# A layer norm's scale and bias on the vector engine instead of GpSimd, and an expert's selection ahead of two subtractions

## The chip, the cores and the metric

The kernel runs on one core of a Trainium2 chip. The metric is the device time of one execution in microseconds (us); the time of a kernel is the median of its runs. The engines are TensorE (PE; PEld is its weight load), VectorE (DVE, here the vector engine), ScalarE (ACT), GpSimd (POOL) and SyncE (SP, which issues most loads).

## The reference, cut to what matters

Two transformer blocks with two layers each are computed one after the other in float32, on 256 tokens of 1024 features. The change touches the second block. Its layer norms, after the residual has been added, and its expert layer are:

```python
for layer in range(DEPTH):
    y = mixer_block(x, ...)
    x = layer_norm(DN_ALPHA * x + y, ln_g[layer, 0], ln_b[layer, 0])
    y = swiglu_2(x, ...) if layer % 2 == 0 else moe_ffn(x, ...)
    x = layer_norm(DN_ALPHA * x + y, ln_g[layer, 1], ln_b[layer, 1])
```

Ahead of the second block the first one ends with an RMS norm with the scale `final_g`. The expert layer routes each token to the best two of 8 experts (hidden width 1408).

## The kernel before, in words

**Split products.** Each float32 product is made of three: every operand is split into a high part, rounded by a cast, and a low part, the difference. For a weight piece, loaded by SyncE into one of the `raw` buffers, the scalar engine makes the high part `whi` (line 233) and the vector engine the low part `wlo` (line 236); in the expert layer each sixth low part is made by GpSimd (`lo_pool = 6`). TensorE then issues the products of lines 342 (high with high), 343 (low weight) and 344 (low state).

**The x state** is a tile `xstate` of 128 x 2 x 1024, two "tokens" t of 128 tokens each. `close` (lines 1624 to 1629) adds the residual, takes the statistics and normalises x in place. What follows reads x in two ways. First, `pre(t)` makes the operand of the next product: `to_feat` turns x by TensorE (line 395), applies the norm's scale and bias by column to the turned tile (line 416 on the vector engine for features 0 to 511, line 412 on the scalar engine for the rest), casts the high parts `xh` (line 388 on the vector engine, line 386 on the scalar engine) and subtracts for the low parts `xl` (line 389). Second, `tok(t)` multiplies x itself by the scale (line 1645) and adds the bias (line 1646), both on GpSimd with rows broadcast to all partitions, for the residual at the end of the layer. The final norm of block 1 has only a scale (line 1696).

**When tok runs.** In `moe` the flag `now` is set and `tok(t)` is issued in `pre(t)`. Otherwise it is put off: `put_off` is a generator in a list of background work, of which the long products (`gemm_tok`) take a step from time to time. The order within each engine's queue is written by a scheduler that goes by priority and by when it thinks inputs are ready; `high_priority` raises what is issued in it, and `issue_after(i)` makes the instructions of a block follow i in the queue of i's engine. `pieces` uses it with `self.made`, the last instruction of the latest `pre`, to keep the weights' splits behind the state's.

There are four places: the mixer of layer 0 (line 1696, put off), the feed-forward of layer 0, the mixer of layer 1 (both lines 1645 and 1646, put off) and the expert layer of layer 1 (the same lines, `now`).

**The expert layer** (`moe`) takes the state's operands, computes the router's logits (line 1757, line 1761), picks the best two (lines 1763 to 1767), ranks the chosen tokens per expert (lines 1770 to 1773, result `rk`), and then stores the split of x as `xth` and `xtl` (lines 386 and 389) for the gather. For an expert e, `gather(e)` compares the ranks with the numbers 1 to 128 (line 1817, the selection `G`) and multiplies `xth` and `xtl` by `G` on TensorE (line 1824). Expert 0 is gathered at once, the others as background work. The list `last` says behind which vector instruction the low part of each stored token is queued; `self.behind` does the same for the first expert's weight splits:

```python
last[0] = last[1]
last[1] = ranked
for t in range(2):
    with tc.issue_after(last[t].ins), tc.issue_after(evac[t].ins):
        self.split(xth[:, t], xtl[:, t], self.x[:, t].rearrange("p (q k) -> p k q", k=KD))
self.behind = last[1]
```

Of the kernel before, what the change touches and what calls it, by code (L numbers as in the profile page):

```python
# [11 lines left out]
F32R = mybir.dt.float32r  # L12
# [3 lines left out]
OP = mybir.AluOpType  # L16
# [3 lines left out]
P = 128  # L20
D = 1024
KD = 8
# [62 lines left out]
class Net:  # L85
# [1547 lines left out]
    def gain(self, L, which, pool, xp, tag="lnb", bufs=2, now=False):  # L1633


        nc, a = self.nc, self.a
        g, b = a["ln_g_2"][L, which], a["ln_b_2"][L, which]
        gb, bb = (self.bcast(v, pool, f"lnb{L}{which}{i}", D, tag=tag, bufs=bufs) for i, v in enumerate((g, b)))
        gf, bf = (self.sp.tile([P, KD], F32, name="lnf", tag="lnf", bufs=4) for _ in range(2))
        nc.gpsimd.dma_start(gf, g.rearrange("(p k) -> p k", k=KD))  # L1640
        nc.gpsimd.dma_start(bf, b.rearrange("(p k) -> p k", k=KD))

        def tok(t):
            z = self.x[:, t]
            nc.gpsimd.tensor_tensor(out=z, in0=z, in1=gb, op=OP.mult)
            nc.gpsimd.tensor_tensor(out=z, in0=z, in1=bb, op=OP.add)

        def pre(t):
            z = self.x[:, t]
            last = self.to_feat(z, KD, xp[t][0], xp[t][1], lambda k: (gf[:, k:k + 1], bf[:, k:k + 1]))  # L1650
            if now:
                tok(t)
            return last
        if not now:
            self.rest = self.put_off(tok)
        return pre

    @staticmethod
    def put_off(tok):
        for t in range(2):  # L1660
            tok(t)
            yield

    def mix_consts(self):
# [20 lines left out]
    def block2_layer0(self):  # L1685
        nc, a, tc = self.nc, self.a, self.tc
        xp = self.xparts()
        fg = self.feat(a["final_g"], self.cp, "final_g")

        def final(pool, xp, tag, bufs):  # L1690
            gb = self.bcast(a["final_g"], pool, "fgb", D, tag=tag, bufs=bufs)

            def pre(t):
                z = self.x[:, t]
                return self.to_feat(z, KD, xp[t][0], xp[t][1], lambda k: (fg[:, k:k + 1], None))
            self.rest = self.put_off(lambda t: nc.gpsimd.tensor_tensor(out=self.x[:, t], in0=self.x[:, t], in1=gb, op=OP.mult))
            return pre
        with ExitStack() as es:
            self.block2_mixer(0, xp, final, es)
            pool = es.enter_context(tc.tile_pool(name="f2", reuse_waits="tile", bufs=1))  # L1700
            xp = self.xparts()
            pre = self.gain(0, 0, pool, xp)
            self.later(iter(range(6)), self.rest)
            lhs = lambda k, t: (xp[t][0][:, k], xp[t][1][:, k])
            w1, w3 = (a[n][0].rearrange("(p k) n -> p k n", k=KD) for n in ("ffn_w1_2", "ffn_w3_2"))
            self.swiglu_tok(lhs, lambda c0, cw: w1[:, :, c0:c0 + cw], lambda c0, cw: w3[:, :, c0:c0 + cw],
                            lambda c0, cw: a["ffn_w2_2"][0][c0:c0 + cw, :].rearrange("(p k) n -> p k n", p=P), 2816, pool,
                            self.close(), pre=pre, nxt=(self.w_in(1), 768, 1024))
            self.extend()
        self.x2parts = self.xparts()  # L1710
        self.load_vec(1)
# [19 lines left out]
    def moe(self, xp, pre, loads, pool):  # L1731

        nc, a, tc = self.nc, self.a, self.tc
        alpha = (2 * 2) ** 0.25
        out = self.dump["x2_1"] if self.out is None else self.out.rearrange("o s d -> (o s) d")
# [3 lines left out]
        tri, iota, rhl, rb = loads  # L1739
        one = self.ones5[:, 0:1]  # L1740
        nc.vector.memset(one, 1.0)
        top2, top, sel, rk, cmb, rkb_ = self.by_expert
# [7 lines left out]
        last, evac = [], []  # L1750
# [14 lines left out]
        for t in range(2):  # L1765
# [6 lines left out]
        nc.tensor.matmul(prk[:, E:2 * E], tri, sel[:, 1], start=False, stop=True)  # L1772
        ranked = nc.vector.scalar_tensor_tensor(out=rk, in0=prk[:, :2 * E].rearrange("p (t e) -> p t e", t=2), scalar=1.0, in1=sel,
                                       op0=OP.add, op1=OP.mult)
        last[0] = last[1]
        last[1] = ranked

        xth, xtl = (pool.tile([P, 2, KD, P], F32R, name=n) for n in ("xth", "xtl"))
        for t in range(2):
# [24 lines left out]
        def experts(base):  # L1804
            rkb = rk
            if base:
                rkb = rkb_
                nc.vector.tensor_scalar(out=rkb, in0=rk, scalar1=-float(base), scalar2=None, op0=OP.add)
            w1, w3 = ([[a[n][0, e].rearrange("(p k) n -> p k n", k=KD)] for e in range(E)] for n in ("exp_w1_2", "exp_w3_2"))
            w2 = [[a["exp_w2_2"][0, e].rearrange("(p k) n -> p k n", p=P)] for e in range(E)]  # L1810
            G, gx, st = {}, {}, {}

            def gather(e):

                G[e] = self.xp.tile([P, 2, P], F32R, name="G", tag="xp", bufs=4)
                for t in range(2):
                    nc.vector.tensor_scalar(out=G[e][:, t], in0=iota, scalar1=rkb[:, t, e:e + 1], scalar2=None, op0=OP.is_equal)
                gh, gl = gx[e] = [pool.tile([P, KD, P], F32R, name=n, tag=n, bufs=2) for n in ("gh", "gl")]
                for k in range(0, KD, 4):
                    for i, (x, d) in enumerate(((xth, gh), (xtl, gl))):  # L1820
                        pg = self.mi().rearrange("p (k n) -> p k n", k=4)
                        for j in range(4):
                            for t in range(2):
                                nc.tensor.matmul(pg[:, j], x[:, t, k + j], G[e][:, t], start=t == 0, stop=t == 1)  # L1824
                        if i:
                            nc.vector.tensor_copy(d[:, k:k + 4], pg)
                        else:
                            nc.scalar.copy(d[:, k:k + 4], pg)
                    yield
# [96 lines left out]
            for e in range(E + 1):  # L1926
                if e < E:
                    if e == 0:
                        for _ in gather(0):
                            pass  # L1930
                        if not base:
                            weights()
                    if e + 1 < E:
                        self.later(gather(e + 1))
                    gs = st["g", e] = pool.tile([P, H], F32, name="gs", tag="gs", bufs=2)
                    up(e, w1, lambda t, b, bw, ps: nc.scalar.activation(gs[:, b:b + bw], ps, AF.Silu),
                       (w2[e - 1], 0, D) if e else (w3[e], 0, H))
                    self.behind = None
                self.finish()
                if e:  # L1940
                    down(e - 1, (w3[e], 0, H) if e < E else None)
                    if e < E:
                        self.later(scatter(e - 1))
                if e < E:
                    self.later(weigh(e))
                    up(e, w3, lambda t, b, bw, ps: nc.vector.tensor_tensor(out=gs[:, b:b + bw], in0=ps, in1=gs[:, b:b + bw],
                                                                           op=OP.mult),
                       (w1[e + 1], 0, H) if e + 1 < E else (w2[e], 0, D))
                    self.finish()
                    self.later(turn(e))  # L1950
            finish()

        stats = [self.sp.tile([P, 2, 6], F32, name="bnst", tag="bnst") for _ in range(2)]
        experts(0)
        _, (most,) = nc.values_load_multi_w_load_instructions(ci[0:1, 0:1], min_val=0, max_val=256)
        with tc.If(most > P):
            experts(P)
# [69 lines left out]
```

## Time and profile before

| | us |
|---|---|
| median of 3 runs | 2438.66 |
| lowest, highest run | 2431.98, 2439.13 |
| profiled execution, its own time | 2432.68 |
| its span | 2430.9 |

In the profiled execution TensorE's granted clock is 0.964 of full speed on average. The profile's page gives for each engine its busy time; its chain of waits goes back from the last instruction to what released it. A timeline row is: start in us, duration in us, engine, line, operation, output<-inputs, shape, count, and in brackets the idle time before it with the instruction that ended it. A row with a count over 1 merges neighbours, and its duration runs from the first one's start to the last one's end.

### The profile page before, as it was taken

The numbers are of one execution on the slowest core, as the hardware profiler recorded it, in microseconds if no ns is written. First come the engines' busy times: TensorE is split into PE (matmuls) and PEld (weight loads), VectorE is DVE, ScalarE is ACT, GpSimd is POOL, SyncE is SP. The second block draws the span as 40 slices with busy tenths as digits, with TensorE's granted clock in tenths as the row PEclk, the third lists the DMA queues.
The fourth block names the chain that finished last, engine by engine and source line by source line (L and its number), as shares of the span: only waits on it lengthen the run. The fifth ranks groups of instructions, "written<-read, shape, count | busy, mean of one in ns | idle before, by whom it ended". The sixth has DMA issues, their size and how long they took to land.

```text
span 2430.9 us, 32300 instructions
## 1 busy us (share of the span) xinstructions
PE 2324.5 (96%) x12726; PEld 1875.9 (77%) x12726; DVE 1483.8 (61%) x2473; ACT 1069.6 (44%) x1700; POOL 309.4 (13%) x245
## 2 busy tenths in 40 slices
PE   8999999999998999999999989989999979999996
PEld 4667887777886778978787768968887768888885
DVE  4248742332357565567465775567566778898787
ACT  3127432222234544434353344423353347777774
POOL 1100000000002010003100210022101222232222
PEclk8989999999999999999998999999999979999998
DMA  8561244454423055644243454634243539889893
GB/s 300 182 191 36 87 156 146 146 183 143 132 83 108 26 180 178 201 138 162 97 139 141 132 185 161 210 112 169 86 155 132 180 127 340 324 317 327 313 343 135
DMA packets 121504, 419.40 MB, mean 173 GB/s; under 512 B 10992, under 2 KB 16112, under 8 KB 110592
## 3 DMA queue, kind: packets, MB, share of 16 engines
q1 hardware_dynamic: 114128, 401.32, 47.0%
q0 software_dynamic: 4832, 15.34, 2.3%
q8 instruction: 102, 1.67, 0.3%
q10 hardware_dynamic: 2384, 0.59, 0.1%
q14 instruction: 58, 0.48, 0.1%
HBM read 416.15 MB, written 1.07 MB: 172 GB/s over the span
## 4 chain that ended last, share of the span: by engine, by line
PE 83%; DVE 9%; issue 3%; POOL 2%; ACT 1%; DMA 1%; SPq 0%; POOLq 0%; ACTq 0%; DVEq 0%
PE acc L342 18%; PE acc L343 18%; PE acc L344 18%; PE acc L375 4%; PE acc L376 3%; PE acc L377 3%; DVE wlo L236 2%; PE mi L1055 2%; PE mi L528 2%; PE mi L540 2%; PE mi L1373 2%; PE mi L395 1%; PE mi L1824 1%; PE mi L1011 1%; PE mi L1039 1%
## 5 line engine op out<-in xcount | busy, mean ns | idle before, releaser
L236 DVE TENSOR_TENSOR wlo<-raw,whi 128x1024 fp32r<-128x1024 f32 (+3 forms) x661 | 797.8, 1234 | 508.0 <-ACT whi L233 502.6
L233 ACT CAST whi<-raw 128x1024 fp32r<-128x1024 f32 (+5 forms) x708 | 675.9, 994 | 710.1 <-PE acc L344 512.4
L342 PE MATMUL acc<-whi,xh 128*128 128x512 f32 (+3 forms) x1184 | 465.4, 396 | 11.6 <-ACT whi L233 4.8
L343 PE MATMUL acc<-wlo,xh 128*128 128x512 f32 (+3 forms) x1184 | 456.8, 386 | 13.1 <-DVE wlo L236 12.8
L344 PE MATMUL acc<-whi,xl 128*128 128x512 f32 (+3 forms) x1184 | 454.0, 384 | 2.2 <-DVE xl L389 2.2
L342 PEld LDWEIGHTS acc<-whi,xh 128*128 128x128 f32 x1184 | 228.4, 193 | 62.5 <-issue 12.0
L343 PEld LDWEIGHTS acc<-wlo,xh 128*128 128x128 f32 x1184 | 227.7, 192 | 55.5 <-DVE wlo L236 21.7
L344 PEld LDWEIGHTS acc<-whi,xl 128*128 128x128 f32 x1184 | 227.4, 192 | 38.3 <-DVE xl L389 3.7
L344 PE MATMUL acc<-whi,hl 128*128 128x512 f32 x528 | 207.6, 393 | 2.2 <-DVE hl L389 2.2
L342 PE MATMUL acc<-whi,hh 128*128 128x512 f32 x528 | 208.1, 394 | 0.0
L343 PE MATMUL acc<-wlo,hh 128*128 128x512 f32 x528 | 207.9, 394 | 0.0
L236 POOL TENSOR_TENSOR wlo<-raw,whi 128x1024 fp32r<-128x1024 f32 (+1 forms) x47 | 119.1, 2534 | 322.2 <-ACT whi L233 322.2
L342 PE MATMUL acc<-whi,gh 128*128 128x512 f32 (+1 forms) x384 | 148.3, 386 | 1.5 <-DVE yl L1886 1.4
L375 PE MATMUL acc<-xh,whi 128*128 128x512 f32 (+1 forms) x384 | 147.0, 384 | 0.0
L376 PE MATMUL acc<-xl,whi 128*128 128x512 f32 (+1 forms) x384 | 145.6, 380 | 0.0
L377 PE MATMUL acc<-xh,wlo 128*128 128x512 f32 (+1 forms) x384 | 145.3, 380 | 0.0
L344 PE MATMUL acc<-whi,gl 128*128 128x512 f32 (+1 forms) x384 | 144.9, 377 | 0.0
L343 PE MATMUL acc<-wlo,gh 128*128 128x512 f32 (+1 forms) x384 | 144.4, 376 | 0.0
L342 PEld LDWEIGHTS acc<-whi,hh 128*128 128x128 f32 x528 | 100.2, 190 | 25.6 <-issue 3.4
L344 PEld LDWEIGHTS acc<-whi,hl 128*128 128x128 f32 x528 | 100.3, 190 | 23.5 <-DVE hl L389 2.6
L343 PEld LDWEIGHTS acc<-wlo,hh 128*128 128x128 f32 x528 | 100.1, 190 | 20.4
L375 PEld LDWEIGHTS acc<-xh,whi 128*128 128x128 f32 x384 | 73.8, 193 | 28.5 <-issue 6.7
(578 smaller groups left out, 3191.5 us busy)
## 6 DMA issues: line engine op xcount, KB each, us to landing
raw<-in_exp_w_dram SPq DMA_DIRECT2D x64, 960.0 KB, 6.3
raw<-in_ada_w_dram SPq DMA_DIRECT2D x48, 1024.0 KB, 5.1
raw<-in_w_in_dram SPq DMA_DIRECT2D x40, 1024.0 KB, 4.7
raw<-in_exp_w_dram SPq DMA_DIRECT2D x40, 1024.0 KB, 6.3
raw<-in_ffn_w_in_dram SPq DMA_DIRECT2D x32, 1024.0 KB, 5.0
raw<-in_exp_w_dram SPq DMA_DIRECT2D x32, 896.0 KB, 5.6
raw<-in_ffn_w_dram SPq DMA_DIRECT2D x27, 1024.0 KB, 4.9
raw<-in_ffn_w_out_dram SPq DMA_DIRECT2D x19, 1024.0 KB, 4.9
```

The costliest lines, as they stand in the source:

```text
L233: nc.scalar.copy(hi, s)
L236: e.tensor_tensor(out=lo, in0=s, in1=hi.bitcast(F32), op=OP.subtract)
L342: nc.tensor.matmul(o, xh, hi(c, m), start=k == 0, stop=False)
L343: nc.tensor.matmul(o, xh, lo(c, m), start=False, stop=False)
L344: nc.tensor.matmul(o, xl, hi(c, m), start=False, stop=k == K - 1 and c + m == b + bw)
L375: nc.tensor.matmul(o, wh, xh[:, n0:n1], start=k == 0, stop=False)
L376: nc.tensor.matmul(o, wh, xl[:, n0:n1], start=False, stop=False)
L377: nc.tensor.matmul(o, wl, xh[:, n0:n1], start=False, stop=k == K - 1)
L528: nc.tensor.matmul(ps[32 * j:32 * j + 32, :], self.ct[:, 4 * g + j, :], v[:, j, :], start=g == 0, stop=g == 1, tile_position=(0, 32 * j))
L540: nc.tensor.matmul(pf[:, 2 * k:2 * k + 2], mod[:, k::KD], self.sel2, start=True, stop=True)
L1055: nc.tensor.matmul(po[:, (h - c0) * 64:(h - c0) * 64 + 64], aT[:, j * P:(j + 1) * P], v(h, jj), start=jj == 0, stop=jj == nkb - 1)
L1373: nc.tensor.matmul(ps[t][rw, h * n:h * n + n], lhsT(m, rw), rhs(m, rw), start=True, stop=True, tile_position=(64 * (cl ^ t), 64 * (cl ^ t)))
```

## The change

The scale and the bias of the x state are applied by the vector engine instead of GpSimd, at all four places. Where they are put off they are queued behind the last instruction of the latest `pre`; in `moe` each is queued behind the split of its own token, and `pre` now returns the addition. The selection `G` of expert 0 is made right behind the ranks, and the low part of the second stored token and the first expert's weight splits are queued behind it instead of behind the ranks; the low part of the first stored token is queued behind the addition of the second token's bias.

```diff
@@ gain
         def tok(t):
             z = self.x[:, t]
-            nc.gpsimd.tensor_tensor(out=z, in0=z, in1=gb, op=OP.mult)
-            nc.gpsimd.tensor_tensor(out=z, in0=z, in1=bb, op=OP.add)
+            nc.vector.tensor_tensor(out=z, in0=z, in1=gb, op=OP.mult)
+            return nc.vector.tensor_tensor(out=z, in0=z, in1=bb, op=OP.add)
 
         def pre(t):
             z = self.x[:, t]
-            last = self.to_feat(z, KD, xp[t][0], xp[t][1], lambda k: (gf[:, k:k + 1], bf[:, k:k + 1]))
+            self.made = self.to_feat(z, KD, xp[t][0], xp[t][1], lambda k: (gf[:, k:k + 1], bf[:, k:k + 1]))
             if now:
+                with self.tc.issue_after(self.made.ins):
+                    return tok(t)
+            return self.made
+        if not now:
+            self.rest = self.put_off(tok, lambda: self.made)
+        return pre
+
+    def put_off(self, tok, after):
+
+        for t in range(2):
+            with self.tc.issue_after(after().ins):
                 tok(t)
-            return last
-        if not now:
-            self.rest = self.put_off(tok)
-        return pre
-
-    @staticmethod
-    def put_off(tok):
-        for t in range(2):
-            tok(t)
             yield
@@ block2_layer0
-            self.rest = self.put_off(lambda t: nc.gpsimd.tensor_tensor(out=self.x[:, t], in0=self.x[:, t], in1=gb, op=OP.mult))
+            self.rest = self.put_off(lambda t: nc.vector.tensor_tensor(out=self.x[:, t], in0=self.x[:, t], in1=gb, op=OP.mult), lambda: self.made)
@@ moe
+        G = {}
+
+        def select(e, rank):
+            G[e] = self.xp.tile([P, 2, P], F32R, name="G", tag="xp", bufs=4)
+            for t in range(2):
+                ins = nc.vector.tensor_scalar(out=G[e][:, t], in0=iota, scalar1=rank[:, t, e:e + 1], scalar2=None, op0=OP.is_equal)
+            return ins
         last[0] = last[1]
-        last[1] = ranked
+        last[1] = select(0, rk)
@@ experts, gather
-            G, gx, st = {}, {}, {}
+            gx, st = {}, {}
...
-                G[e] = self.xp.tile([P, 2, P], F32R, name="G", tag="xp", bufs=4)
-                for t in range(2):
-                    nc.vector.tensor_scalar(out=G[e][:, t], in0=iota, scalar1=rkb[:, t, e:e + 1], scalar2=None, op0=OP.is_equal)
+                if e or base:
+                    select(e, rkb)
```

## Rows read from the trace of the kernel before

**Rows 1.** The chain that ended last, by engine.

```profile
PE 83%; DVE 9%; issue 3%; POOL 2%; ACT 1%; DMA 1%; SPq 0%; POOLq 0%; ACTq 0%; DVEq 0%
```

**Rows 2.** Stretches: length, PE, PEld, DVE, ACT, POOL busy (instructions); PEclk, DMA, GB/s.

```profile
1415.00:1420.00 5.00, 2.57 (x8) 1.61 (x6) 5.00 (x6) 3.66 (x4) 0.97 (x1) 0.80 0.00 0
...
1990.00:2415.00 425.00, 417.79 (x2083) 358.62 (x2081) 359.11 (x359) 299.96 (x359) 116.28 (x46) 1.00 0.83 306
1435.00:1602.00 167.00, 167.00 (x803) 144.73 (x802) 84.97 (x88) 73.59 (x89) 0.00 (x0) 1.00 0.57 194
```

**Rows 3.** Timeline of GpSimd, feed-forward of layer 0.

```profile
1413.51 2.46 POOL L1646 TENSOR_TENSOR xstate<-xstate,lnb 128x1024 f32<-128x1024 f32 x1
```

**Rows 4.** Timeline of the vector engine, feed-forward of layer 0.

```profile
1412.51 1.21 DVE L388 CAST xh<-xt 128x512 fp32r<-128x512 f32 x1
1413.75 2.77 DVE L389 TENSOR_TENSOR xl<-xt,xh 128x512 fp32r<-128x512 f32 x1
1416.44 1.21 DVE L236 TENSOR_TENSOR wlo<-raw,whi 128x1024 fp32r<-128x1024 f32 x1
...
1425.86 2.51 DVE L236 TENSOR_TENSOR wlo<-raw,whi 128x1024 fp32r<-128x1024 f32 x1
1428.29 2.58 DVE L388 CAST xh<-xt 128x512 fp32r<-128x512 f32 x1
...
1436.28 4.63 DVE L236 TENSOR_TENSOR wlo<-raw,whi 128x1024 fp32r<-128x1024 f32 x4 [1.93 <-ACT whi L233]
```

**Rows 5.** Timeline of the vector engine, mixer of layer 1.

```profile
1611.34 0.43 DVE L388 CAST xh<-xt 128x512 fp32r<-128x512 f32 x1
1611.80 0.69 DVE L389 TENSOR_TENSOR xl<-xt,xh 128x512 fp32r<-128x512 f32 x1
...
1616.75 2.35 DVE L1111 TENSOR_SCALAR nsinks<-vec 128x8 f32<-128x8 f32 x1
...
1624.13 2.62 DVE L236 TENSOR_TENSOR wlo<-raw,whi 128x1024 fp32r<-128x1024 f32 x1
1626.67 2.59 DVE L388 CAST xh<-xt 128x512 fp32r<-128x512 f32 x1
1629.19 3.44 DVE L389 TENSOR_TENSOR xl<-xt,xh 128x512 fp32r<-128x512 f32 x2
1638.56 2.36 DVE L236 TENSOR_TENSOR wlo<-raw,whi 128x1024 fp32r<-128x1024 f32 x2 [5.94 <-ACT whi L233]
```

**Rows 6.** Timeline of TensorE, feed-forward of layer 0.

```profile
1432.13 0.50 PE L344 MATMUL acc<-whi,xl 128*128 128x512 f32 x1 [0.22 <-DVE xl L389]
```

**Rows 7.** Timeline of GpSimd, mixer of layer 1.

```profile
1616.66 2.40 POOL L1645 TENSOR_TENSOR xstate<-xstate,lnb 128x1024 f32<-128x1024 f32 x1
...
1625.63 5.85 POOL L1646 TENSOR_TENSOR xstate<-xstate,lnb 128x1024 f32<-128x1024 f32 x2
```

**Rows 8.** Timeline of the vector engine, expert layer.

```profile
1949.74 3.36 DVE L389 TENSOR_TENSOR xl<-xt,xh 128x512 fp32r<-128x512 f32 x2
...
1960.13 2.12 DVE L388 CAST xh<-xt 128x512 fp32r<-128x512 f32 x1
1962.28 5.47 DVE L389 TENSOR_TENSOR xl<-xt,xh 128x512 fp32r<-128x512 f32 x2
...
1972.52 1.99 DVE L389 TENSOR_TENSOR xtl<-xstate,xth 128x1024 fp32r<-128x1024 f32 x1
1974.42 0.47 DVE L1817 TENSOR_SCALAR G<-b_iota,rk 128x128 fp32r<-128x128 bf16 x2
```

**Rows 9.** Timeline of GpSimd, expert layer.

```profile
1964.41 2.79 POOL L236 TENSOR_TENSOR wlo<-raw,whi 128x1024 fp32r<-128x1024 f32 x1
```

**Rows 10.** Timeline of the scalar engine, expert layer.

```profile
1961.12 0.62 ACT L386 CAST xh<-xt 128x512 fp32r<-128x512 f32 x1
```

**Rows 11.** Timeline of TensorE, the first expert's gather.

```profile
1974.75 2.02 PE L1824 MATMUL mi<-G,xth 128*128 128x128 f32 x8 [2.37 <-DVE G L1817]
```

**Rows 12.** Timeline of the vector engine, mixer of layer 0.

```profile
1098.29 8.65 DVE L236 TENSOR_TENSOR wlo<-raw,whi 128x1024 fp32r<-128x1024 f32 x4 [3.27 <-ACT whi L233]
```

## The prediction

> **What bounds the kernel now.** I read the chain of waits first: TensorE holds 83% of it and the vector engine 9% [rows 1]. The long weight products are TensorE's own time, and only the 9% can be touched here. Next the stretches [rows 2]: from 1435 to 1602 us TensorE is busy for 167.00 of 167 us, and in the experts' part for 417.79 of 425 us at a DMA share of 0.83. So time won ahead of these parts should reach the end. In 1415 to 1420 us it is the other way round: the vector engine has 5.00 of 5.00 us, TensorE 2.57. Such short stretches stand where the x state passes a layer norm, at three places: the feed-forward of layer 0 (I call it B), the mixer of layer 1 (C) and the expert layer (D). The mixer of layer 0 (A) has a single multiplication by the final norm's scale.
>
> Then the order in time of GpSimd and of the vector engine at B. GpSimd's addition runs from 1413.51 to 1415.97 us [rows 3]. The 512-column subtraction that starts beside it at 1413.75 ends at 1416.52, 0.55 us after GpSimd let go, and has cost 2.77 us [rows 4]. At C the same cast and the same subtraction of the first token have no GpSimd arithmetic beside them and cost 0.43 and 0.69 us [rows 5]. So a vector operation that reads two tiles of SBUF, or casts from SBUF to SBUF, stands still until GpSimd's 2.4 us operation is over. At B every such operation of the split stands still in turn, and TensorE's first product of the second token with its low part starts when the vector engine's subtraction lets it, at 1432.13 [rows 6].
>
> **The change, part by part.** Twelve GpSimd operations (six multiplications, six additions, on 128x1024) and the two of A become 14 vector operations, queued behind the split of their token or, at A, B and C, of the second token. Price of one: the weights' low-part subtraction has the same shape and two SBUF inputs, and took 1.21 us once GpSimd was quiet [rows 4]. That is 17 us of new vector work in all. What GpSimd's stops cost today:
>
> B, with the quiet prices of C [rows 4, 5]: cast of the first token 1.21-0.43 = 0.78; its first subtraction 2.77-0.69 = 2.08; a weight subtraction 2.51-1.21 = 1.30; cast of the second token 2.58-0.43 = 2.15. Together 6.3. Some of TensorE's own products lie between, so I take **6.0**.
>
> C [rows 5]: the vector engine's 8-column operation of 2.35 us, which starts inside GpSimd's multiplication of 1616.66 to 1619.06 [rows 7], should cost no more than the 512-column cast, and I take 2.2 as gone; weight subtraction 2.62-1.21 = 1.41; cast 2.59-0.43 = 2.16; two subtractions 3.44-2x0.69 = 2.06, beside GpSimd's two additions of 5.85 us [rows 7]. Together 7.8; I take **7.5**.
>
> D [rows 8]: cast of the second token 2.12-0.43 = 1.69; its two subtractions 5.47-2x0.69 = 4.09, of which the second waits for GpSimd's weight subtraction that starts at 1964.41 [rows 9] behind the norm's addition. Together 5.8. The scalar engine's half of the cast ends at 1961.74 [rows 10], which would then be the later input, so 5.4. The selection G starts at 1974.42 behind the second stored low part (1.99 us, from 1972.52) [rows 8]; placed ahead it wins 1.9. The two vector operations of the second token (2.4 us) now stand where the first stored low part stood (2.0 us, the same shape as the second), -0.4. Both stored low parts come later; the first should fit into the vector engine's wait for the ranks for some 0.5 us, and the gather's second group of products, which needs them 1.8 us after the gather starts at 1974.75 [rows 11], should wait some 0.4. That leaves **6.0**.
>
> The first token's stop at D (3.36 us for two subtractions, 1.98 over the quiet price [rows 8]) I count at nothing: its own two operations, 2.4 us, can now stand there instead, ahead of the second token's residual and statistics. Bounds: 2.0 won if they stand later, 2.4 lost if GpSimd's weight subtraction, which no longer queues behind the norm, moves up and stops one of them. I take zero because the two known sums are nearly equal.
>
> Where the new operations hide. At C the vector engine has 5.94 us idle behind the split [rows 5], more than 4x1.21 = 4.8. At B the next gap is 1.93 us [rows 4], and gaps like it follow; if the scheduler puts all four ahead of the next weight subtractions, TensorE waits up to 4.8 less the 1.2 us that two more products of the held pieces give, 3.6 us. I take zero, since these operations are issued late in the program and their x state is not read before the layer's end; the 3.6 stays for the range. At A [rows 12] four subtractions took 8.65 us where 4x1.21 = 4.8 is their price; the loss is 3.8 us and the new work 2.4, and TensorE did not show it, so zero. GpSimd's queue loses work only; nothing on it gets later. SyncE's loads wait for raw buffers, which the weight subtractions free; they move with the splits. On the scalar engine the high part of the first stored token waits for the new addition, and behind it stand the second token's scaled columns: that is part of the bound of 2.4.
>
> Sum: 6.0+7.5+6.0 = 19.5 us. The profiled execution took 2432.68 us (span 2430.9), near the low end of the runs, whose median is 2438.66. From its own time the sum gives 2413.2, from the median 2419.2; I forecast **2415**.
>
> A rule that speaks against it: the vector engine is full in just these stretches [rows 2]. The Trainium skill (Perfetto Trace Analysis, Optimizing Scalar/DVE Operations) says that work of a saturated vector engine may be moved to the scalar engine or even to GpSimd, and adds that the two share a read port so that it may not help. By its first half the change goes the wrong way, which is the third rival below; the rows of B against C speak for its second half.
>
> **The rivals.**
> 1. *The new order costs half at B and D.* All four operations ahead of the weight subtractions at B (-3.6), GpSimd's subtraction among D's vector work (-2.4), both stored low parts behind G and the gather waiting for one of them (-2.0): 19.5-8.0 = 11.5, so 2421. For it: the order is the scheduler's and can't be read from this trace. Against: the vector engine's gaps [rows 4, 5].
> 2. *The work moves into the place of the stops.* All operations of B, C and D stand on the path: 12x1.21 = 14.5 us against 19.5, some 5 won, 2428 from the profile, 2434 from the median: hardly to be told from no change. For it: D's first token looks like that. Against: only the first two at D have something urgent behind them.
> 3. *Slower: the vector engine is the bound, and its long operations are long for another reason than GpSimd.* Then nothing is won, and the 14.5 us stand on the path: 2432.7+14.5 = 2447. It decides at one row: whether a 512-column subtraction behind a transposed token takes 0.69 or 2.8 us with GpSimd idle. The quiet token of C [rows 5] speaks clearly against it.
> 4. That the operations don't stay behind the splits is a variant of rival 2: the order is tied to the last split's low part, and nothing in the rows says otherwise.
>
> **How the numbers follow.** A measurement of this kernel tells about 0.3% (7 us) from no change. Forecast 0.70, rival 1 0.15, rivals 2 and 4 0.10, rival 3 0.05. Faster by over 0.3% are the forecast and rival 1: 0.85; within 0.3% rival 2: 0.10; slower rival 3: 0.05. Low end: from 2413.2, 2.0 more at D, the rest of B's and C's terms (0.6), and 1 us at each of the three places for products at the lower clock behind the stops (the granted clock was 0.80 in 1415 to 1420 [rows 2], a fifth of 5 us, where I counted no gain) give 2407.6; a run at the low end of the spread gives 2405. High end: rival 1 counted from the median, 2438.7-11.5 = 2427, and a little of rival 2: 2429. The range leaves out rival 3 and most of rival 2.
>
> **What would show it.** Right: in the changed profile all casts of a split at B, C and D take 0.43 us and all 512-column subtractions 0.69; the new operations take 1.2 us each and lie behind the second token's split; TensorE's waits for low parts at B and C fall to below 1 us; G comes right behind the ranks, and the gather starts about 19 us earlier than 1974.75, counted from the start. Wrong: operations of 1.2 us ahead of the second token's statistics or of weight subtractions on which TensorE then waits; a GpSimd weight subtraction inside D's split; a gather that stands before the stored low parts; or vector operations as long as before with GpSimd idle.

## The result and the profile after

The changed kernel takes 2409.75 us (median of 4 runs, 2407.31 to 2412.49) against 2438.89 us for the kernel before (median of 4). The ratio is 0.9887 with a 95% interval of 0.9867 to 0.9908, so it is faster by 27.6 us between the means (22 to 32). Forecast were 2415 us and a range of 2405 to 2429. The profiled execution took 2412.49 us and has a span of 2410.7 us, 20.2 less than the 2430.9 of before. The gap between 20.2 and 27.6 lies in the choice of the profiled executions: that of before is 4.7 us faster than the mean of its runs, that of after 2.7 us slower; it is taken up below.

The page of after, first its busy times, then the chain that ended last by engine:

```profile
PE 2318.2 (96%) x12726; PEld 1874.0 (78%) x12726; DVE 1472.6 (61%) x2487; ACT 1069.2 (44%) x1700; POOL 273.8 (11%) x231
...
PE 84%; DVE 8%; issue 3%; POOL 2%; ACT 1%; DMA 1%; SPq 0%; POOLq 0%; ACTq 0%; DVEq 0%
```

The vector engine has 14 instructions and some 17 us of work more than before, and yet is busy for 11.2 us less (1483.8 before): the new work has replaced about 28 us of standing still. In the chain one hundredth went from the vector engine to TensorE [rows 1].

To see where the 20.2 us went, both spans are divided at the same instructions: the first transposition of A, the first residual of B, C and D (line 1624), the end of the second token's low parts there, and the first product of the gather. The lengths between them:

| stretch | before | after | difference | forecast |
|---|---|---|---|---|
| start to A | 1078.2 | 1078.7 | +0.5 | 0 |
| A to B (final norm, mixer of layer 0) | 325.6 | 319.6 | -6.0 | 0 |
| B, to the end of the split | 28.3 | 22.1 | -6.2 | -6.0 |
| B to C (long products) | 170.6 | 170.6 | 0 | 0 |
| C, to the end of the split | 30.0 | 22.1 | -7.9 | -7.5 |
| C to D (mixer of layer 1) | 307.2 | 309.9 | +2.7 | 0 |
| D, to the gather | 35.0 | 31.0 | -4.0 | -6.0 |
| gather to the end | 456.2 | 456.8 | +0.6 | 0 |

**B and C.** The vector engine of after in order of time, first B and then C:

```profile
1406.96 0.43 DVE L388 CAST xh<-xt 128x512 fp32r<-128x512 f32 x1
1407.42 0.69 DVE L389 TENSOR_TENSOR xl<-xt,xh 128x512 fp32r<-128x512 f32 x1
...
1418.73 0.42 DVE L388 CAST xh<-xt 128x512 fp32r<-128x512 f32 x1
1419.07 1.28 DVE L389 TENSOR_TENSOR xl<-xt,xh 128x512 fp32r<-128x512 f32 x2
1420.27 2.35 DVE L236 TENSOR_TENSOR wlo<-raw,whi 128x1024 fp32r<-128x1024 f32 x2
1422.54 2.35 DVE L1645 TENSOR_TENSOR xstate<-xstate,lnb 128x1024 f32<-128x1024 f32 x2
...
1427.08 6.90 DVE L236 TENSOR_TENSOR wlo<-raw,whi 128x1024 fp32r<-128x1024 f32 x6
...
1605.04 0.12 DVE L1111 TENSOR_SCALAR nsinks<-vec 128x8 f32<-128x8 f32 x1
...
1611.41 0.42 DVE L388 CAST xh<-xt 128x512 fp32r<-128x512 f32 x1
1611.74 1.28 DVE L389 TENSOR_TENSOR xl<-xt,xh 128x512 fp32r<-128x512 f32 x2
1612.95 2.35 DVE L1645 TENSOR_TENSOR xstate<-xstate,lnb 128x1024 f32<-128x1024 f32 x2
...
1617.49 4.62 DVE L236 TENSOR_TENSOR wlo<-raw,whi 128x1024 fp32r<-128x1024 f32 x4
```

The cast that took 1.21 and 2.58 us at B and 2.59 at C [rows 4, 5] takes 0.42 or 0.43; the subtraction of 2.77 takes 0.69; the 8-column operation of 2.35 at C takes 0.12. The four new operations lie behind the split of the second token and cost 1.2 us each. At B they stand ahead of six weight subtractions, the place that the forecast had kept as its bound of 3.6 us. They cost nothing there: the second of these windows of after (columns as in [rows 2]), in which they lie, shows TensorE busy for 170.00 of 170 us. In the first, which holds the split, it is busy for 21.20 of 25:

```profile
1397.00:1422.00 25.00, 21.20 (x98) 16.54 (x97) 22.55 (x52) 9.82 (x16) 1.07 (x2) 1.00 0.37 125
...
1420.00:1590.00 170.00, 170.00 (x816) 147.19 (x815) 91.92 (x95) 73.57 (x89) 0.53 (x1) 1.00 0.57 199
```

TensorE's waits at B, first before, then after. Only 2.0 us for weights' low parts and the wait for the normalised x (1.4 before) are left; at C 2.1 us for weights' low parts are left, and none for the state's parts:

```profile
PE acc L343 <- DVE wlo L236: 4.7, 3, 2.4
PE acc L342 <- DVE xh L388: 1.3, 1, 1.3
PE acc L344 <- DVE xl L389: 0.2, 1, 0.2
...
PE acc L343 <- DVE wlo L236: 2.0, 2, 1.3
PE mi L395 <- DVE xstate L1629: 1.8, 2, 1.4
```

TensorE's granted clock differs there too. Windows of before around B and C:

```profile
1403.00:1433.00 30.00, 22.34 (x93) 16.24 (x92) 28.07 (x51) 9.82 (x16) 12.08 (x7) 0.94 0.32 109
1602.00:1639.00 37.00, 27.61 (x108) 20.59 (x107) 29.22 (x52) 9.46 (x16) 14.35 (x11) 0.86 0.21 67
```

TensorE stood still for 7.7 of the 30 us and 9.4 of the 37, and the clock fell to the lower of its two levels (1.2 and 2.4 GHz) for a part of both; these are means over both levels. After, it is 1.00 at both places. All ten traces agree: the clock fell at B and at C in the four kernels in which GpSimd works beside the splits there (before, experiments 3, 4 and 8) and in none of the six others. What this is worth is not measured apart from the stops.

**D.** The vector engine of after at the expert layer:

```profile
1933.70 1.22 DVE L1645 TENSOR_TENSOR xstate<-xstate,lnb 128x1024 f32<-128x1024 f32 x1
1934.84 0.68 DVE L1624 SCALAR_TENSOR_TENSOR xstate<-xstate,acc 128x512 f32<-128x512 f32 x1
1935.43 1.22 DVE L1646 TENSOR_TENSOR xstate<-xstate,lnb 128x1024 f32<-128x1024 f32 x1
...
1937.53 1.36 DVE L461 SCALAR_TENSOR_TENSOR rv<-bnmv,quart 128x3 f32<-128x3 f32 x1
...
1944.13 0.43 DVE L388 CAST xh<-xt 128x512 fp32r<-128x512 f32 x1
...
1948.84 2.00 DVE L389 TENSOR_TENSOR xtl<-xstate,xth 128x1024 fp32r<-128x1024 f32 x1
1950.75 0.24 DVE L1765 MAX8 top<-mi 128x8 f32<-128x8 f32 x2
...
1953.36 0.17 DVE L1775 SCALAR_TENSOR_TENSOR rk<-mi,sel 128x16 f32<-128x16 f32 x1 [1.38 <-PE mi L1774]
```

GpSimd and TensorE of after at the same place:

```profile
1935.77 3.11 POOL L236 TENSOR_TENSOR wlo<-raw,whi 128x1024 fp32r<-128x1024 f32 x1 [17.15 <-ACT whi L233]
...
1953.93 2.01 PE L1832 MATMUL mi<-G,xth 128*128 128x128 f32 x8 [0.61 <-DVE G L1782]
1955.74 2.12 PE L1832 MATMUL mi<-G,xtl 128*128 128x128 f32 x8
```

The cast is quiet (0.43 for 2.12 [rows 8]) and the gather starts at 1953.93 instead of 1974.75 [rows 11]. But two rows are not as forecast. The first stored low part (1948.84) stands ahead of the router's maxima, not in the wait for the ranks; that wait, 1.38 us, is still there, empty. And GpSimd's weight subtraction has moved up to 1935.77, beside the statistics of the second token: a 3-column operation takes 1.36 us there. TensorE shows the first of these as a wait for the choice of experts, 3.3 us where it was 1.2 (waits at D, before and after):

```profile
PE mi L1770 <- DVE sel L1767: 1.2, 1, 1.2
...
PE mi L1772 <- DVE sel L1769: 3.3, 1, 3.3
```

**The two mixers.** The rest of the balance, -6.0 and +2.7, lies where the kernel was hardly changed. At A the vector engine copies the first projection out 1.6 us earlier (27.0 us behind A's start instead of 28.7), and TensorE's own work is 1.4 us earlier from there on. One of its rows in before, after and experiment 1, with A's start at 1078.20, 1078.67 and 1082.06, so 70.6, 69.3 and 69.5 us behind it:

```profile
1148.84 0.41 PE L1337 MATMUL mi<-diag,AZ 128*128 128x128 f32 x2 [0.23 <-DVE AZ L1322]
...
1147.93 0.41 PE L1337 MATMUL mi<-diag,AZ 128*128 128x128 f32 x2 [0.22 <-DVE AZ L1322]
...
1151.53 0.41 PE L1337 MATMUL mi<-diag,AZ 128*128 128x128 f32 x2 [0.22 <-DVE AZ L1322]
```

The other 4.6 us come later, in the mixer itself, and there TensorE's clock is what differs. Windows of before, 10 us each, the same place in the mixer of layer 0 and then of layer 1 (column behind the engines: granted clock):

```profile
1270.00:1280.00 10.00, 10.00 (x41) 7.13 (x40) 5.50 (x11) 5.21 (x15) 1.46 (x1) 0.73 0.77 303
1280.00:1290.00 10.00, 10.00 (x39) 6.22 (x37) 8.29 (x12) 5.13 (x9) 0.55 (x1) 0.84 0.50 170
1290.00:1300.00 10.00, 10.00 (x35) 7.21 (x35) 1.56 (x5) 1.51 (x5) 0.00 (x0) 0.57 0.31 106
...
1810.00:1820.00 10.00, 10.00 (x53) 7.58 (x52) 7.35 (x16) 6.34 (x18) 2.49 (x3) 1.00 0.71 277
```

The same places of after:

```profile
1268.50:1278.50 10.00, 10.00 (x53) 7.59 (x52) 7.35 (x16) 6.34 (x17) 2.50 (x3) 1.00 0.72 277
1278.50:1288.50 10.00, 10.00 (x39) 5.85 (x38) 7.39 (x11) 4.09 (x8) 0.09 (x1) 0.85 0.73 240
1288.50:1298.50 10.00, 10.00 (x50) 8.43 (x50) 1.80 (x6) 2.70 (x7) 0.00 (x0) 0.81 0.15 61
...
1789.00:1799.00 10.00, 10.00 (x41) 7.23 (x40) 5.61 (x12) 5.38 (x15) 1.57 (x1) 0.76 0.76 297
```

TensorE is busy without a gap in all of them. In these two traces a stretch comes in two shapes: 0.73, 0.84, 0.57, which is 8.6 us short of full speed in 30, and 1.00, 0.85, 0.81, which is 3.4. Before had the long one in layer 0 and the short one in layer 1 (its other two windows, not shown, 0.88 and 0.78); after has them the other way round (0.84 and 0.55). Each exchange is worth about 5 us.

### The profile page after: what moved, and what is told of

Read it like the earlier page. It is cut to its first block, busy times and chain, and to the rows that moved or that the text cites. A ratio compares the mean times of both kernels' runs of the same rounds, so it can differ in the third digit from the quotient of the medians.

```text
span 2410.7 us, 32287 instructions
## 1 busy us (share of the span) xinstructions
PE 2318.2 (96%) x12726; PEld 1874.0 (78%) x12726; DVE 1472.6 (61%) x2487; ACT 1069.2 (44%) x1700; POOL 273.8 (11%) x231
## 4 chain that ended last, share of the span: by engine, by line
PE 84%; DVE 8%; issue 3%; POOL 2%; ACT 1%; DMA 1%; SPq 0%; POOLq 0%; ACTq 0%; DVEq 0%
PE acc L342 19%; PE acc L343 18%; PE acc L344 18%; PE acc L375 4%; PE acc L376 3%; PE acc L377 3%; DVE wlo L236 2%; PE mi L1055 2%; PE mi L528 2%; PE mi L540 2%; PE mi L1373 2%; PE mi L395 1%; PE mi L1832 1%; PE mi L1011 1%; PE mi L1039 1%
## 5 line engine op out<-in xcount | busy, mean ns | idle before, releaser
L236 DVE TENSOR_TENSOR wlo<-raw,whi 128x1024 fp32r<-128x1024 f32 (+3 forms) x661 | 789.7, 1221 | 497.9 <-ACT whi L233 492.6
```

What stands on the lines that cost most here:

```text
L236: e.tensor_tensor(out=lo, in0=s, in1=hi.bitcast(F32), op=OP.subtract)
```

## The experiments

**Theory:** GpSimd's arithmetic beside the splits holds up the vector engine, and nothing else about the old place of the work costs anything at B and C. **Rivals:** the engine matters in itself (late GpSimd operations still stop vector operations on which TensorE waits); the gain is the selection's new order; A or the clock brings it. For D: the first stored low part and the first token's two operations stand in the way. The times of before are the medians of runs on the same chip.

**1. GpSimd keeps the work at A, B and C but does it late.** GpSimd reads one column of the second token's last low part first, so its operations start when the split is done. D as in the changed kernel.

```diff
+        eng = nc.vector if now else nc.gpsimd
         def tok(t):
-            nc.vector.tensor_tensor(out=z, in0=z, in1=gb, op=OP.mult)
-            return nc.vector.tensor_tensor(out=z, in0=z, in1=bb, op=OP.add)
+            eng.tensor_tensor(out=z, in0=z, in1=gb, op=OP.mult)
+            return eng.tensor_tensor(out=z, in0=z, in1=bb, op=OP.add)
...
+    def mark(self, xl):
+        c = self.sp.tile([P, 1], F32, name="cw", tag="cw")
+        self.marked = self.nc.gpsimd.tensor_copy(c, xl[:, KD - 1, P - 1:P].bitcast(F32))
```

> The put-off scale and bias (places A, B, C) stay on GpSimd, but wait there for the second token's split by a one-column read of its last low part; place D is as in the changed kernel. Theory (GpSimd's arithmetic beside the splits blocks them; which engine does the work later is of no account): the casts of the splits at B and C take 0.43 us and the subtractions 0.69, B and C win as much as in the changed kernel (6.2 and 9.8 us), GpSimd's 2.4 us operations stop weight subtractions later that have slack; ratio 0.989 to 0.991. Rival (the gain needs the vector engine's 1.2 us instead of GpSimd's 2.4): the weight subtractions stopped behind the splits hold TensorE, B and C win at most half, ratio 0.993 to 0.997.

Measured: 2415.65 us, ratio to before 0.9908 (0.9881 to 0.9934). B lasts 22.1 us and C 22.1, to a tenth what they last in the changed kernel. GpSimd and the vector engine of this kernel at B:

```profile
1424.17 0.58 POOL L1665 COPY cw<-xl 128x1 f32<-128x1 f32 x1 [0.35 <-DVE xl L389]
1424.72 6.76 POOL L1647 TENSOR_TENSOR xstate<-xstate,lnb 128x1024 f32<-128x1024 f32 x2
...
1423.43 1.27 DVE L389 TENSOR_TENSOR xl<-xt,xh 128x512 fp32r<-128x512 f32 x2
1424.63 18.05 DVE L236 TENSOR_TENSOR wlo<-raw,whi 128x1024 fp32r<-128x1024 f32 x8
```

The stops are there as before: eight weight subtractions take 18.05 us (2.26 each instead of 1.2), and GpSimd's operations take 3.4 us each. But TensorE's waits for weights at B are the same 2.0 us in two. So at B and C the engine that does the work does not matter; its time beside the split does. The theory holds and the first rival falls. At A the first projection came out only at 29.7 us behind A's start, not 27.0, but that held up the vector engine's copy alone: TensorE's own work is within 0.2 us of the changed kernel's (row above). The median is 5.9 us above that of the changed kernel; between the two profiled executions it is 3.6, of which 3.4 lie ahead of A, where both have the same code.

The Trainium skill (SBUF — State Buffer, Who interferes with whom) says that the vector engine's second port pair is GpSimd's only one, held for a whole instruction, and that a vector operation with two SBUF inputs contends with a GpSimd instruction that reads SBUF. The rows of B agree, and they show both sides being held up in turn.

**2. Only A, B and C moved; D as before.**

```diff
+        eng = nc.gpsimd if now else nc.vector
```

> Only the put-off places A, B, C on the vector engine; the expert layer D (norm on GpSimd, selection behind the stored low parts) as before. Theory: what B and C won in the changed kernel stays, up to the start of D 16 to 17 us, and D takes its 35.0 us from its first residual to the first gather as before; span about 2415 us, ratio about 0.991. Rival (D gives most of it, the rest is chance of the clock in the mixers): ratio above 0.995.

Measured: 2411.12 us, 0.9894 (0.9871 to 0.9917). B and C last 22.1 us, D 35.0 as before. Most of the gain is here.

**3. Only D as in the changed kernel.**

```diff
+        eng = nc.vector if now else nc.gpsimd
```

> Only the expert layer D as in the changed kernel; A, B, C on GpSimd as before. Theory: B takes its 30 us and C its 37 us of before, D wins 4.0 us from its first residual to the first gather (31.0 instead of 35.0); span about 2427, ratio 0.998. Rival (D's gain needs the earlier places too, or is worth more): span below 2422.

Measured: 2430.87 us, 0.9979 (0.9961 to 0.9996), so 1 to 9.5 us. D lasts 31.0 us to the gather, B and C 28.3 and 30.0 as before. By the place D is worth 4.0 us; the whole time agrees but does not size it.

**4. Only the selection's new order.**

```diff
-        last[1] = ranked
+        last[1] = select(0, rk)
```

> The kernel before, with expert 0's selection ahead of the second stored low part as the only edit. Theory: the selection starts 1.9 us earlier from D's first residual (32.7 instead of 34.6 us) and the gather too, nothing else moves: ratio 0.999. Rival (the gather then waits for the second stored low part, 1.99 us, and gives it all back): the third group of gather products starts no earlier, ratio 1.000.

Measured: 2433.64 us, 0.9987 (0.9971 to 1.0004), not to be told from no change. The place shows it: the gather starts 33.15 us behind D's start instead of 34.96, so 1.8 us are won. TensorE of this kernel:

```profile
1980.41 2.01 PE L1830 MATMUL mi<-G,xth 128*128 128x128 f32 x8 [0.59 <-DVE G L1780]
1982.23 2.12 PE L1830 MATMUL mi<-G,xtl 128*128 128x128 f32 x8
```

The rows with `xtl` follow without a gap, so its late subtraction costs 0.2 us at most (2.12 against 1.9 to 2.0 of the rows with `xth`). Its profiled span is 2437.3 us, 6.4 longer than before, with the same order of work up to D: B lasts 29.0 us instead of 28.3, B to C 171.9 instead of 170.6, C 30.6 instead of 30.0, and C to D 312.3 instead of 307.2. That is the clock, in a kernel that changes nothing there: its mean is 0.86 instead of 0.94 at B and 0.81 instead of 0.86 at C.

**5. The first stored low part behind the choice of experts.** On the changed kernel, so that it can only fall into the wait for the ranks.

```diff
+        chosen = nc.vector.tensor_scalar(out=sel, in0=sel, scalar1=-3e38, scalar2=None, op0=OP.is_equal)
-        last[0] = last[1]
+        last[0] = chosen
```

> The changed kernel, with the first stored low part queued behind the choice of the two experts instead of behind the second token's bias. Theory (the 2.0 us low part stood ahead of the router's maxima and cost nearly all of itself): the maxima start 1.9 us earlier, the low part fills the 1.4 us wait for the ranks and loses 0.6 there; first gather 29.7 us after D's first residual instead of 31.0. Rival (the scalar engine or the gather waits for the low part instead): 31.0 stays.

Measured: 2407.42 us, 0.9876 (0.9860 to 0.9893). The gather starts 29.4 us behind D's start instead of 31.0. The vector engine of this kernel:

```profile
1942.95 0.24 DVE L1765 MAX8 top<-mi 128x8 f32<-128x8 f32 x2
...
1943.92 2.01 DVE L389 TENSOR_TENSOR xtl<-xstate,xth 128x1024 fp32r<-128x1024 f32 x1
1945.86 0.15 DVE L1775 SCALAR_TENSOR_TENSOR rk<-mi,sel 128x16 f32<-128x16 f32 x1
```

This is the order that the forecast had assumed, and the 1.6 us are the price of the other one. The ranks now follow the choice by 2.02 us (1943.84 to 1945.86) where it was 1.72 in the changed kernel (1951.64 to 1953.36), so the low part costs 0.3 us here; the forecast had 0.5.

**6. Also the first token's scale and bias behind the second token's normalisation.**

```diff
-                with self.tc.issue_after(self.made.ins):
+                with self.tc.issue_after(self.made.ins), self.tc.issue_after(self.closed.ins):
                     return tok(t)
```

> As the run before, and at D the first token's scale and bias are also queued behind the second token's normalisation. Theory (these two operations, 2.4 us, stood ahead of the second token's statistics): the normalisation ends 2.4 us earlier; one of the two operations hides behind the transposes' 1.2 us, the other costs 1.2, so the first gather comes at 28.5 us. Rival (the first token's stored high part on the scalar engine becomes late and holds the second token's columns): 29.7 or later.

Measured: 2405.67 us, 0.9869 (0.9853 to 0.9886). The second token's split ends 22.7 us behind D's start instead of 23.6, but the gather starts only 0.25 us earlier (29.1). The vector engine of this kernel shows both reasons:

```profile
1930.51 1.87 DVE L191 SCALAR_TENSOR_TENSOR rs_t<-rs_i,rv 128x1 f32<-128x1 f32 x1
...
1942.85 0.25 DVE L1765 MAX8 top<-mi 128x8 f32<-128x8 f32 x2 [0.52 <-PE mi L1763]
```

GpSimd's weight subtraction (1930.03 to 1932.37 us here) now stops a one-column operation of the norm for 1.87 us; the same operation takes 0.22 elsewhere. And the maxima, which came straight behind other vector work in experiment 5, now wait 0.52 us for the router's logits from TensorE.

**7. Also no weight subtraction on GpSimd until the first expert's first products are done.**

```diff
-        self.lo_pool = 6
...
                     self.behind = None
+                    self.lo_pool = 6
```

> As the run before, and GpSimd takes no weight subtraction before the first expert's first products are issued. Theory (GpSimd's weight subtraction stops the vector engine once between the second token's statistics, 1.36 us for a 3-column operation): that stop goes, the first gather comes at 27.3 us; the rest of the experts as before. Rival (the weight subtraction that the vector engine then does itself makes the first expert wait): gather earlier, but the stretch from the gather to the end longer by as much.

Measured: 2404.46 us (2402.47 to 2405.04), 0.9862 (0.9846 to 0.9879), the lowest of all, though its interval overlaps that of the changed kernel. The gather starts 27.5 us behind D's start. The vector engine of this kernel:

```profile
1929.43 0.16 DVE L461 SCALAR_TENSOR_TENSOR rv<-bnmv,quart 128x3 f32<-128x3 f32 x1
...
1941.67 2.00 DVE L389 TENSOR_TENSOR xtl<-xstate,xth 128x1024 fp32r<-128x1024 f32 x1
```

GpSimd does nothing at D any more, every small operation is short, TensorE waits for the choice of experts for 1.2 us, as in experiment 6 and before the change, and the gather comes 1.65 us earlier than in experiment 6. By this place alone the version beats the changed kernel by 3.5 us; from the gather to the end it gives 0.8 back against experiment 6, presumably for the subtractions that the vector engine took over (not tried apart).

**8. Only the final norm's scale at A moved.**

```diff
-            self.rest = self.put_off(lambda t: nc.gpsimd.tensor_tensor(out=self.x[:, t], in0=self.x[:, t], in1=gb, op=OP.mult))
+            self.rest = self.put_off(lambda t: nc.vector.tensor_tensor(out=self.x[:, t], in0=self.x[:, t], in1=gb, op=OP.mult), lambda: self.made)
```

> Only place A (the final norm's scale in the mixer of layer 0) on the vector engine, all else as before. Theory (A shifts the later work of the mixer of layer 0 by about 1.4 us, and with it the stretches of TensorE's low clock there): B starts near 1398 us with some 10 us of low clock ahead of it, instead of 1403.8 and 20.5; B, C and D take 28.3, 30.0 and 35.0 us as before. Rival (A is worth nothing and the shorter low stretch was chance): B starts near 1403 with 20 us of low clock.

Measured: 2433.09 us, 0.9979 (0.9969 to 0.9988), so 3 to 7.5 us are won at a place that the forecast counted at nothing. A to B lasts 321.3 us against 325.6, and the first projection comes 27.1 us behind A's start. The interval of A to B over all kernels is plain: 325.6 to 325.8 us in the three that leave A as it was (before, experiments 3 and 4), 319.6 to 321.3 in the seven others. In the same seven, experiment 1 too, TensorE's row at 70.6 us behind A comes at 69.3 to 69.5. The clock goes with it: in the first of the three windows at that place in the mixer of layer 0 it is 0.70 to 0.74 in the three kernels, and 1.00 in the changed one and in experiments 1, 2, 5 and 8. So the theory's link, an earlier TensorE and a shorter stretch of the lower clock, holds in all ten traces, but why 1.2 to 1.4 us decide it no run shows.

The rest did not stay as expected. B lasts 29.1 us, C 30.6 and C to D 312.3, nearly as in experiment 4, so this profiled execution (2433.64 us) is no shorter than that of before: what was won at A went again further on. The 5.1 us stand on the whole times alone.

## Why the prediction was right, and where it was not

**The total.** The time, 2409.75, lies inside the range and 5 us below the forecast. The direction, the mechanism and the terms of B and C held; two were off, A and D, with opposite signs, so that the total comes out as near as it does is in part luck.

**B and C, right.** -6.2 and -7.9 us against 6.0 and 7.5. The quiet prices of C's first token [rows 5] were those that came. That C's 8-column operation was held by GpSimd, and not by its own work, is borne out at 0.12 us. Experiment 1 shows that the cause is GpSimd's time beside the split. One sign that the forecast named did not come: TensorE's waits for low parts should have fallen below 1 us, and for weights' low parts 2.0 us are left at B and 2.1 at C. The lower clock at B and C, of which the forecast kept 1 us a place in its range, is gone.

**The cover at B and C, right.** The four operations cost nothing, at C in the idle time behind the split and at B ahead of weight subtractions. There the forecast named the wrong cover, the gaps; what hides them is slack in the weight subtractions themselves: experiment 1 makes eight of them nearly twice as long, and TensorE waits no longer.

**D, mis-sized by 2.0 us.** Two steps failed. "the first should fit into the vector engine's wait for the ranks for some 0.5 us": nothing tied the first stored low part to that place, it was put ahead of the maxima and cost its full length; experiment 5 got 1.6 us back by tying it. "The first token's stop at D [...] I count at nothing": the second token's split came only 4.4 us earlier instead of 5.4, as the first token's two operations and GpSimd's subtraction, which moved up as the bound of 2.4 said it might, stood ahead of the second token's statistics. Experiments 6 and 7 together took 2.5 us of its split time out (23.6 to 21.1) and 1.9 us ahead of the gather (29.4 to 27.5). The term for the selection held: 1.8 us in experiment 4 against 1.9. The gather's wait for the stored low parts was 0.2, not 0.4.

**A, failed.** "TensorE did not show it, so zero": the profile of before did show it, as 1.3 us of TensorE's waits for weights' low parts at A against 0.5 after, a row that the forecast did not read; it read the vector engine's row [rows 12] alone. Experiment 8 measures 5.1 us (3 to 7.5) for A. The direct part is 1.4 on TensorE, of which these waits are 0.8; the rest goes with the clock, whose shape was read but not set by any run.

**Profile and runs.** The sum was made from the profile's own 2432.68, and the forecast put between that and the median. The terms as measured, 5.1 at A, 6.2, 7.9 and 4.0, make 23.2 of the 27.6 us; the first is a whole time, the others are lengths in one profiled execution each. The remaining 4.4 lie inside the interval (22 to 32). The runs of before differ by 14 us, and their mean granted clocks with them (2425.92 us at 0.967, 2432.84 at 0.964, 2439.83 at 0.959); the changed kernel's lie between 2407 and 2412 at 0.966 to 0.968. Experiment 4's profiled execution, 2439.04 us at 0.960, has the code of before up to D, and against the profile of before it is 7.9 us longer from the start of B to that of D, all of it in stretches with more of the lower clock. So the rest may be low clock at B, at C and in the mixer of layer 1 that most runs of before have and its profiled one has less of; those runs left no trace, so this is not shown.

**The rivals.** Rival 1's order came at B, without its price, and half of it came at D, for 2.0 us. Rivals 2 and 3 fell at the rows that were named for them: with GpSimd idle a 512-column subtraction takes 0.69 us, and only at D did new operations stand on the path. The rule of the Trainium skill that spoke against the change (Perfetto Trace Analysis, Optimizing Scalar/DVE Operations) had two halves; its second, that sharing a port may undo the gain of GpSimd, agrees with these runs: GpSimd's operations beside the splits cost more than the same work on the vector engine behind them.

## What to carry to other kernels

Arithmetic that is handed to GpSimd "for free" can be paid by what the vector engine does meanwhile; look for one vector operation with two durations, price the difference, and move the work either to the vector engine behind what is urgent or to a later time on GpSimd, which was worth the same at two places here. Where a scheduler writes the order of a queue, an operation that is meant to fill a wait must be tied behind what it must not delay, or it may take the place ahead of it. And measure a change of a few us between fixed instructions of the trace: the whole time of one and the same code moved by up to 14 us with the clock.

## What was not expected of the hardware

- Very small vector operations can be held as long as large ones: 3 columns 1.36 us for 0.16, one column 1.87 for 0.22, 8 columns 2.35 for 0.12, each beside one GpSimd operation. Not all are: in experiment 6 two one-column integer operations beside the same GpSimd operation took 0.15 each. In a chain of small operations, as a norm has, one held operation stops the whole chain.
- GpSimd pays as well: 2.4 us for a 128x1024 operation with a quiet neighbour [rows 7], 3.4 us beside weight subtractions that follow each other.
- TensorE's granted clock falls in the middle of both mixers while it is busy without a gap, in a long and a short shape that differ by 5 us in before and after, and in shapes between them in other runs (0.74, 0.84, 0.74 in experiment 4). Kernels that differ by 1.2 to 1.4 us ahead of it in layer 0 show different shapes. C to D, nearly the same work in all kernels, took from 305.2 to 312.3 us.
